# Four of sixteen new sample states moved from the second FFN into the mixer, and one weight quarter moved from a DMA to VectorE

## The chip, the cores and the metric

The kernel runs on one core of a Trainium2 chip. A core has five engines with a queue each: TensorE (PE in the profile; PEld is its weight load), VectorE (DVE), ScalarE (ACT), GpSimd (POOL) and SyncE (SP), which here only issues DMAs. POOL issues DMAs too, and it alone issues the accumulating ones, which add what they bring to what lies in the target. Each queue is worked off in order. The metric is the device time of one execution in microseconds (us); shorter is better.

## The reference

One inference step of a hybrid decoder trunk, in float32: half a SwiGLU FFN, a mixer, half a SwiGLU FFN, and a final RMSNorm. It runs for 512 prompt positions and for 8 sample sequences of one new token each; the kernel treats both together as 520 columns.

```python
h = h + 0.5 * _swiglu(_rms_norm(h, ffn1_norm), ffn1_w_gate, ffn1_w_up, ffn1_w_down)   # 1024 -> 2816 -> 1024
h = h + mixer(_rms_norm(h, mix_norm))      # in-projection, pooling, causal conv, SSD scan, gate, out-projection
h = h + 0.5 * _swiglu(_rms_norm(h, ffn2_norm), ffn2_w_gate, ffn2_w_up, ffn2_w_down)
y = _rms_norm(h, final_norm)
```

What the change touches is one output, the new recurrent state of the samples. For each sample b and each of 16 heads of 64 rows, with N = 128 state columns,

```
new_state[b] = exp(-dt * A) * state[b] + (dt * x) outer B[b]
y_sample[b]  = new_state[b] . C[b] + ...
```

The kernel holds a sample's state as 8 tiles of 128 x 128 (two heads in each). The names are `sdec` for the decay, one number for each partition, tile and sample, `sxdt` for dt * x, and a row of B that is broadcast to all partitions. The kernel computes `y_sample` without the new state, from the old one and from the dot product of B and C, so nothing on the chip reads the new state: it goes to the output `nss`.

## The kernel before

**Matrix products.** Every weight is split in two parts, a high part (a cast to the matmul's format, on ACT) and a low part (what the cast lost), and so are the activations. A product takes three matmuls: high x high, high x low, low x high (`mm3`, lines 146, 149 and 150). 520 columns are two halves of 260, one matmul each. The low part of a weight is either a subtraction on DVE (L136, L237, L384) or made by DMA: ACT copies the high part negated, and an accumulating DMA on POOL's queue adds the original from memory (`part_by_dma` L230, and L382).

**The FFNs.** Each FFN goes through 22 tiles of 128 hidden rows in chunks of 8, 8 and 6 (`CHUNKS`). After the first and the second chunk come four down products each, `Down(0,d)` and `Down(1,d)`; the last chunk's down products come at the end (`down_by_half`). A tile combines its two column halves and its two halves of the contraction with sums and differences, so that seven products do the work of eight (`product(f, p)`, p from 1 to 7); sums of weights are made on DVE (L412, L414, L415). The product with p = 4 uses one quarter of the weights; it is made late, in `quarter(f)`, and is multiplied within the next tile. `LOW_BY_DMA` lists the tiles whose quarter gets its low part by DMA: for the second FFN, tiles 0 to 6, 9 and 11.

Raw weights arrive over SP's queue into two buffers of 1 MB in turn, so a tile's load waits until the tile two before it has been split. The partial sums leave PSUM by copies on ACT (L476) and sums on DVE (L480, L485).

**The mixer.** Three strings, `CONV_PLAN`, `GATE_PLAN` and `LAST_PLAN`, give the order in which the program is written down: one letter and a number for each step. `b`, `x`, `p`, `z` are in-projections (24 units of weights), `A` and `B` the two halves of a scan step for a chunk of 128 positions and a group of heads (`ssd_a`, `ssd_b`), `s2` two sample steps (`sample`, L1088), `G` and `H` the gate, `o`, `g`, `h` out-projections, `n` a part of the second FFN's first tile that fills in. A planner then puts each engine's queue in order: in a simulated time it issues what is ready, the earliest written first. What is marked `keep_in_program_order` keeps its order among its like.

A sample step loads a row of C and half a sample's state (4 tiles, 256 KB) over SP, multiplies them on DVE (L1094), and sums each tile along its columns on ACT (L1097); that ACTIVATE's own output is not needed and goes to a tile `junk`, which shares its place (the tag "acc") with the FFNs' square sums.

**New sample states.** `new_states` (L1109) is a generator in the second FFN. Its 16 states are halves of samples, (b, g), 256 KB each. POOL's queue loads the row of B (64 KB) and the old state. Four ACTIVATEs write row x `sxdt` (L1139), four DVE instructions compute state x `sdec` + that (L1141), and a store goes out on POOL's queue (L1143). The loads run up to two states ahead, and the tile `room` has two places. `STATES` says when the generator moves on by one state: in `stream` (L534) the tuple's first member gives the number of states at each Down product by its d, the second lists tiles, and the third counts the first down products of the last chunk. The first call only loads. So before, the generator is started at tile 6, makes one state at each of the eight Down products, one each at tiles 17, 19, 20 and 21, and four at the end.

Of the kernel before, what the change touches and what calls it, by code (L numbers as in the profile page):

```python
# [10 lines left out]
F32 = mybir.dt.float32  # L11
F32R = mybir.dt.float32r
AF = mybir.ActivationFunctionType
ALU = mybir.AluOpType
# [3 lines left out]
P = 128  # L18
D = 1024
SEQ = 512  # L20
NS = 8
NT = SEQ + NS
# [12 lines left out]
CHUNKS = (8, 8, 6)  # L35
LOW_ON_DVE = ((2, 0), (3, 0), (KF - 1, 1))
ON_ACT = 4
STATES = ((1, 1, 1, 1), (6, 17, 19, 20, 21), 4)
LOW_BY_DMA = {1: (2, 3, 4, 5, 6), 2: (*range(7), 9, 11)}

CONV_PLAN = (
    "b0 b1 d0 b2 b3 x0 x1 v0 d1 x2 x3 d2 X0 p0 y0 c0 A0 k0 p1 x4 m0 x5 B0 c1 p2 m1 A1 x6 c2 A2 B1 x7 X1 m2 A3"
)
GATE_PLAN = (
    "z0 B2 A4 z1 B3 p3 z2 B4 s2 z3 c3 A5 s2 z4 m3 B5 s2 A6 z5 e0 s2 G0 z6 A7 z7 B6 s2 o0 H0 s2 o1 B7 s2 o2 s2 G1 "
    "o3 g0 g1 H1 g2 g3"
)
LAST_PLAN = "h0 h2 h1 n0 h3 n1 n2 n3"
SAMPLE_U = 3 + SEQ
# [14 lines left out]
def tile_trunk_step(ctx: ExitStack, tc: tile.TileContext, ins: dict, outs: dict):  # L64
    nc = tc.nc
# [5 lines left out]
    act = ctx.enter_context(tc.tile_pool(name="act", bufs=1, side="left"))  # L71
# [184 lines left out]
    class Ffn:  # L256
# [277 lines left out]
        def stream(self, before, last_chunk):  # L534
            tiles = []
            for f in range(self.direct, KF):
                tiles.append(f)
                if f and f <= self.folded and f % CHUNKS[0] == 0:
                    tiles.extend(Down(f // CHUNKS[0] - 1, d) for d in range(KD // 2))
            prev = None  # L540
            for t in tiles:
                for _ in range(STATES[0][t.d] if not isinstance(t, int) else t in STATES[1]):
                    next(self.states, None)
                self.product(t, 1)
                if prev is not None:
                    self.product(prev, 4)
                for k, p in enumerate((2, 5, 6, 3, 7) if t in (2, KF - 1) else (5, 6, 3, 7, 2)):
                    if k == 1 and prev is not None:
                        self.close(prev)
                    self.product(t, p)  # L550
                self.gates(t)
                if t == 5 and self.later:
                    with queued(*ends[1:]):
                        self.later.pop()()
                prev = t
            self.product(KF - 1, 4)
            with tc.high_priority():
                self.close(KF - 1)
            wd = before()
            if wd is None:  # L560
                self.down(len(CHUNKS) - 1, self.folded, KF, last_chunk)
            else:
                self.down_by_half(len(CHUNKS) - 1, self.folded, last_chunk, wd)
# [48 lines left out]
        def down_by_half(self, c, lo, after, wd):  # L612
            n = KF - lo
            banks, units = {}, []
            for d in range(KD):
                if d < STATES[2]:
                    next(self.states)
# [46 lines left out]
    wx1, g1 = pool("wx1", "right"), pool("g1", "right")  # L664
# [116 lines left out]
    g2 = f2["ffn"].gp = pool("g2", "left")  # L781
# [16 lines left out]
    todo, late = [], []  # L798
# [49 lines left out]
def mixer(tc, ins, outs, e):  # L848
    nc = tc.nc
    cst, act, wp, tmp, dr, pool = (e[x] for x in ("cst", "act", "wp", "tmp", "dr", "pool"))  # L850
# [4 lines left out]
    xh, xl, _, r = nx2[0]  # L855
    xa = e["xa"][0]
    mp = pool("mx", "right")
# [191 lines left out]
    sdec = cst.tile([P, NX, NS], F32, tag="sdec", name="sdec")  # L1049
    sxdt = cst.tile([P, NX, NS], F32, tag="sxdt", name="sxdt")  # L1050
    ysm = mp.tile([P, NX, NS], F32, tag="ysm", name="ysm")
    sbc = mp.tile([P, 2, NS], F32, tag="sbc", name="sbc")
    junk = act.tile([P, NT], F32, tag="acc", name="junk")[:, :P]
    scr_bc = dr.tile([NS, 512], F32, name="scr_bc")

    def rows_bc(b, a, g):
        return scr_bc.rearrange("b (a g n) -> b a g n", a=2, g=2)[b, a, g].unsqueeze(0).to_broadcast([P, P])
# [30 lines left out]
    def sample(b, g):  # L1088
        cb = tmp.tile([P, HB], F32, tag="ta", name=f"cb{b}{g}")[:, :P]
        nc.sync.dma_start(out=cb, in_=rows_bc(b, 1, g))  # L1090
        h0 = mp.tile([P, 4, P], F32, tag="h0", bufs=4, name=f"h0_{b}{g}")
        nc.sync.dma_start(out=h0, in_=ins["state_ssm"][:, b, 4 * g : 4 * g + 4])
        tc.keep_in_program_order(
            nc.vector.tensor_tensor(out=h0, in0=h0, in1=cb.unsqueeze(1).to_broadcast([P, 4, P]), op=ALU.mult))  # L1094
        for q in range(4):
            tc.keep_in_program_order(
                nc.scalar.activation(out=junk, in_=h0[:, q], func=AF.Copy,  # L1097
                                     accum_out=ysm[:, 4 * g + q, b : b + 1]))

    def sample_y(g):  # L1100
# [8 lines left out]
    def new_states(room):  # L1109
        spare = [room.rearrange("p (a q n) -> p a q n", a=2, q=4)] * 2  # L1110

        def load(b, g):
            if "hg" in f2:
                br = f2["hg"].tile([P, P], F32, tag="br", bufs=3, name=f"br{b}{g}")
                hs = f2["hg"].tile([P, 4, P], F32, tag="hs", bufs=3, name=f"hs{b}{g}")
            else:
                br = tmp.tile([P, HB], F32, tag="ta", name=f"br{b}{g}")[:, :P]
                hs = spare[g][:, b % 2]
            tc.keep_in_program_order(nc.gpsimd.dma_start(out=br, in_=rows_bc(b, 0, g)))
            tc.keep_in_program_order(nc.gpsimd.dma_start(out=hs, in_=ins["state_ssm"][:, b, 4 * g : 4 * g + 4]))  # L1120
            return br, hs

        todo = [(b, g) for g in range(2) for b in range(NS)]
        ahead = []
        for i, (b, g) in enumerate(todo):
            if not ahead:
                ahead.append(load(b, g))
            yield
            while i + len(ahead) < len(todo) and len(ahead) < 2 + 2 * ("hg" in f2):
                ahead.append(load(*todo[i + len(ahead)]))  # L1130
            br, hs = ahead.pop(0)
            if "hg" in f2:
                o = f2["hg"].tile([P, 4, P], F32, tag="so", bufs=2, name=f"so{b}{g}")
            else:
                o = bank(f"so{b}{g}").rearrange("p (q n) -> p q n", q=4)
            for q in range(4):
                j = 4 * g + q
                tc.keep_in_program_order(
                    nc.scalar.activation(out=o[:, q], in_=br, func=AF.Copy, scale=sxdt[:, j, b : b + 1]))  # L1139
                tc.keep_in_program_order(  # L1140
                    nc.vector.scalar_tensor_tensor(out=hs[:, q], in0=hs[:, q], scalar=sdec[:, j, b : b + 1],  # L1141
                                                   in1=o[:, q], op0=ALU.mult, op1=ALU.add))
            tc.keep_in_program_order(nc.gpsimd.dma_start(out=outs["nss"][:, b, 4 * g : 4 * g + 4], in_=hs))  # L1143
        yield

    e["f2"]["states"] = new_states


# [137 lines left out]
    def outs_a():  # L1286
        nc.sync.dma_start(out=outs["ncp"], in_=ncp)
        nc.sync.dma_start(out=outs["ncs"], in_=sconv)
        nc.sync.dma_start(out=outs["npp"], in_=npp)
        nc.sync.dma_start(out=outs["nps"], in_=spool)  # L1290
# [20 lines left out]
        "h": lambda j: wout(cats[1], 2, j, fin),  # L1311
        "n": fill,
        "e": lambda j: outs_a(),
    }

    def run(plan):
# [98 lines left out]
```

## Time and profile before

| | before |
|---|---|
| time, median of 3 runs | 964.78 us (963.81 to 965.73) |
| profiled execution | 965.28 us |
| its span, first to last instruction | 963.5 us |
| granted TensorE clock | 0.997 |
| busy PE / DVE / ACT / POOL | 99% / 88% / 66% / 15% |
| mixer, by TensorE's work | about 340 to 615 us |
| second FFN, tiles 1 to 8 | about 618 to 699 us |
| Down(0,0) to Down(0,3) | about 700 to 742 us |
| tiles 9 to 16, then Down(1,0) to Down(1,3) | about 742 to 824, to 865 us |

The profile is of one execution. A row of the timeline has the start, the duration, engine and line, output and inputs, and in brackets how long the engine stood idle before it and for whom. A matmul is shown with a modelled end and overlaps the next one, so a gap is read from start to start. A busy TensorE in a stretch can still have lost time; the count of matmuls in it says more.

### The profile page before, as it was taken

How to read it: one execution, taken by the hardware profiler on the slowest of the kernel's cores; microseconds unless marked ns; L12 is line 12 of the kernel's file. 1: busy time of each engine (PE TensorE's matmuls, PEld its weight loads, DVE VectorE, ACT ScalarE, POOL GpSimd, SP SyncE). 2: the span in 40 equal slices, each digit the busy share in tenths (PEclk: the TensorE clock that was granted, in tenths of full speed). 3: DMA queues.
4: the chain of work that ended last, by engine and by line, in shares of the span. 5: the costliest groups of instructions: out<-in, count | busy, mean ns of one | idle time of the engine just before them, and what ended most of it. 6: DMA issues, size and time to landing. Idle time of an engine off the chain costs nothing.

```text
span 963.5 us, 19707 instructions
## 1 busy us (share of the span) xinstructions
PE 949.7 (99%) x7676; PEld 930.3 (97%) x7676; DVE 850.3 (88%) x1456; ACT 640.7 (66%) x1208; POOL 142.9 (15%) x228
## 2 busy tenths in 40 slices
PE   9999999999999999999999999999999999999995
PEld 8999999999999999999999999999999999999995
DVE  6899899998997788789978897999889999999886
ACT  7777656676566455485676565677676676766763
POOL 0111101001010001055241000112112101122120
PEclk9999999999999999999999999999999999999998
DMA  7665654545534243362353333447656655666642
GB/s 210 182 167 145 152 156 111 138 136 143 163 112 129 73 142 110 94 199 92 117 159 121 115 117 114 117 121 166 170 154 178 154 146 147 166 192 174 187 141 90
DMA packets 53631, 137.30 MB, mean 142 GB/s; under 512 B 7641, under 2 KB 15769, under 8 KB 53537
## 3 DMA queue, kind: packets, MB, share of 16 engines
q1 hardware_dynamic: 39840, 104.18, 33.4%
q0 software_dynamic: 13424, 31.73, 17.2%
q8 instruction: 60, 0.98, 0.4%
q14 instruction: 35, 0.28, 0.1%
q10 hardware_dynamic: 272, 0.13, 0.0%
HBM read 128.67 MB, written 7.34 MB: 141 GB/s over the span
## 4 chain that ended last, share of the span: by engine, by line
PE 29%; DVE 11%; issue 4%; ACT 3%; DMA 3%; POOL 0%; DVEq 0%; ACTq 0%; POOLq 0%
PE A L150 3%; PE A L146 3%; PE A L149 3%; PE BE L149 3%; PE BE L146 2%; PE BE L150 2%; DMA raw<-in_w2d 2%; PE wo L146 2%; PE wo L150 2%; PE wo L149 2%; PE dh L150 1%; PE dh L146 1%; PE dh L149 1%; ACT junk L1097 1%; PE P L295 1%
## 5 line engine op out<-in xcount | busy, mean ns | idle before, releaser
L476 ACT COPY ac<-A 128x260 f32<-128x260 f32 x85 | 31.7, 373 | 34.8 <-PE A L150 33.6
L412 DVE TENSOR_TENSOR s<-raw 128x1024 f32<-128x1024 f32 x39 | 47.5, 1219 | 2.9 <-DMA raw<-in_w1gu 1.3
L476 ACT COPY ac<-BE 128x260 f32<-128x260 f32 x41 | 15.4, 376 | 30.0 <-PE BE L150 29.0
L146 PE MATMUL inx<-xh_mx,whi_inx 128*128 128x260 f32 x112 | 31.8, 284 | 0.0
L149 PE MATMUL inx<-xl_mx,whi_inx 128*128 128x260 f32 x112 | 31.6, 282 | 0.0
L150 PE MATMUL inx<-xh_mx,wlo_inx 128*128 128x260 f32 x112 | 31.6, 282 | 0.0
L977 DVE SCALAR_TENSOR_TENSOR A<-U,h,A 128x544 f32<-128x544 f32 x36 | 28.9, 802 | 1.3 <-ACT A L975 0.9
L295 PE MATMUL P<-x,raw 128*128 128x260 f32 x128 | 28.6, 384 | 0.0
L295 PEld LDWEIGHTS P<-x,raw 128*128 128x128 f32 x128 | 24.2, 191 | 4.0 <-DMA raw<-in_w1gu 0.4
L146 PE MATMUL wo<-catg,whi_wo 128*128 128x260 f32 x96 | 27.7, 289 | 0.0
L150 PE MATMUL wo<-catg,wlo_wo 128*128 128x260 f32 x96 | 27.2, 284 | 0.0
L149 PE MATMUL wo<-catg,whi_wo 128*128 128x260 f32 x96 | 27.1, 282 | 0.0
L1097 ACT ACTIVATE junk<-h 128x128 f32<-128x128 f32 x64 | 19.8, 309 | 10.5 <-DVE h L1094 9.0
L1139 ACT ACTIVATE so<-br,sxdt 128x128 f32<-128x128 f32 x64 | 22.5, 375 | 4.6 <-DVE room L1141 4.6
L150 PE MATMUL A<-xth_f,qs 128*128 128x260 f32 x84 | 23.8, 283 | 0.7 <-DMA qs<-in_w2gu 0.7
L146 PE MATMUL A<-xth_f,qs 128*128 128x260 f32 x84 | 23.8, 284 | 0.0
L1240 DVE TENSOR_TENSOR h<-wo,h 128x260 f32<-128x260 f32 x48 | 19.0, 416 | 5.4 <-PE wo L150 5.4
L149 PE MATMUL A<-xtl_f,qs 128*128 128x260 f32 x84 | 23.7, 282 | 0.0
L237 DVE TENSOR_TENSOR gs<-gq,gs 128x780 fp32r<-128x780 f32 (+1 forms) x28 | 23.2, 827 | 0.4 <-ACT gs L236 0.4
L146 PE MATMUL inz<-xh_mx,whi_inz 128*128 128x260 f32 x80 | 22.9, 287 | 0.0
L149 PE MATMUL inz<-xl_mx,whi_inz 128*128 128x260 f32 x80 | 22.7, 283 | 0.0
L150 PE MATMUL inz<-xh_mx,wlo_inz 128*128 128x260 f32 x80 | 22.6, 283 | 0.0
(2529 smaller groups left out, 4745.6 us busy)
## 6 DMA issues: line engine op xcount, KB each, us to landing
raw<-in_w2gu SPq DMA_DIRECT2D x44, 512.0 KB, 4.1
raw<-in_w1gu SPq DMA_DIRECT2D x41, 512.0 KB, 4.2
raw<-in_w_in SPq DMA_DIRECT2D x24, 512.0 KB, 3.6
raw<-in_w1d SPq DMA_DIRECT2D x16, 512.0 KB, 4.5
raw<-in_w2d SPq DMA_DIRECT2D x16, 512.0 KB, 4.8
raw<-in_w_out SPq DMA_DIRECT2D x12, 512.0 KB, 3.7
ab<-scr_acs SPq DMA_DIRECT2D x8, 512.0 KB, 5.0
h<-in_state_ssm SPq DMA_DIRECT2D x16, 256.0 KB, 3.3
```

Of the source, the lines that this page charges most:

```text
L146: first = nc.tensor.matmul(ps, whi, xhi, start=start, stop=False, **kw)
L149: nc.tensor.matmul(ps, whi, xlo, start=False, stop=False, **kw)
L150: nc.tensor.matmul(ps, wlo, xhi, start=False, stop=stop, **kw)
L237: low = nc.vector.tensor_tensor(out=lo, in0=s, in1=hi.bitcast(F32), op=ALU.subtract)
L295: mm = nc.tensor.matmul(self.banks[f, u][b][:, :HB], ws(self.raw[f][:, u], j + 4 * q), xg[:, slot[q]], start=j == q == 0, stop=j == 3 and ...
L412: nc.vector.tensor_tensor(out=s1, in0=diag, in1=up0, op=ALU.add)
L476: self.copied = nc.scalar.copy(keep, out[:, :HB]).ins
L977: nc.vector.scalar_tensor_tensor(out=A[:, :n], in0=U[:, j : j + n], scalar=w(j), in1=A[:, :n], op0=ALU.mult, op1=ALU.add)
L1097: nc.scalar.activation(out=junk, in_=h0[:, q], func=AF.Copy, accum_out=ysm[:, 4 * g + q, b : b + 1]))
L1139: nc.scalar.activation(out=o[:, q], in_=br, func=AF.Copy, scale=sxdt[:, j, b : b + 1]))
L1240: nc.vector.tensor_tensor(out=h[:, d, hs], in0=ps[:, :HB], in1=h[:, d, hs], op=ALU.add)
```

## The change

Four of the 16 states, b = 0 to 3 of the first half, are no longer made in the second FFN. A new generator, `first_states`, makes them in the mixer, moved on by the new step `t` in `GATE_PLAN`, nine times. For each state SP loads the row of B and the old state; after a projection ACT scales the row by `sxdt` into a tile `o`, and the old state by `sdec` in place; POOL issues an accumulating DMA from `o` to the state; after another projection SP stores it, and goes on with the next state's loads into the same two tiles. `o` takes the place that `junk` had, and so the sample steps' sums now write their unneeded output over their own input.

In the second FFN the generator starts with the fifth state, at tile 15. `STATES[0]` is now indexed by the chunk: none at Down(0,d), one at each Down(1,d). Tiles 17, 19, 20, 21 and the last down products make the same states as before. Tile 9 leaves `LOW_BY_DMA`, so the low part of its quarter is subtracted on DVE.

```diff
-STATES = ((1, 1, 1, 1), (6, 17, 19, 20, 21), 4)
-LOW_BY_DMA = {1: (2, 3, 4, 5, 6), 2: (*range(7), 9, 11)}
+FIRST = 4
+STATES = ((0, 1), (15, 17, 19, 20, 21), 4)
+LOW_BY_DMA = {1: (2, 3, 4, 5, 6), 2: (*range(7), 11)}
 
 GATE_PLAN = (
-    "z0 B2 A4 z1 B3 p3 z2 B4 s2 z3 c3 A5 s2 z4 m3 B5 s2 A6 z5 e0 s2 G0 z6 A7 z7 B6 s2 o0 H0 s2 o1 B7 s2 o2 s2 G1 "
-    "o3 g0 g1 H1 g2 g3"
+    "t0 z0 t0 B2 A4 z1 t0 B3 p3 z2 t0 B4 s2 z3 t0 c3 A5 s2 z4 t0 m3 B5 s2 A6 z5 t0 e0 s2 G0 z6 t0 A7 z7 B6 t0 s2 o0 H0 s2 o1 "
+    "B7 s2 o2 s2 G1 o3 g0 g1 H1 g2 g3"
 )
...
-                for _ in range(STATES[0][t.d] if not isinstance(t, int) else t in STATES[1]):
+                for _ in range(STATES[0][t.c] if not isinstance(t, int) else t in STATES[1]):
...
-    junk = act.tile([P, NT], F32, tag="acc", name="junk")[:, :P]
...
-                nc.scalar.activation(out=junk, in_=h0[:, q], func=AF.Copy,
+                nc.scalar.activation(out=h0[:, q], in_=h0[:, q], func=AF.Copy,
                                      accum_out=ysm[:, 4 * g + q, b : b + 1]))
...
-        todo = [(b, g) for g in range(2) for b in range(NS)]
+        todo = [(b, g) for g in range(2) for b in range(NS)][FIRST:]
...
+    def first_states():
+        for b in range(FIRST):
+            br = mp.tile([P, P], F32, tag="mb", name=f"mb{b}")
+            hs = mp.tile([P, 4, P], F32, tag="mh", name=f"mh{b}")
+            nc.sync.dma_start(out=br, in_=rows_bc(b, 0, 0))
+            nc.sync.dma_start(out=hs, in_=ins["state_ssm"][:, b, :4])
+            yield
+            o = act.tile([P, NT], F32, tag="acc", name=f"mo{b}")[:, : 4 * P].rearrange("p (q n) -> p q n", q=4)
+            for q in range(4):
+                nc.scalar.activation(out=o[:, q], in_=br, func=AF.Copy, scale=sxdt[:, q, b : b + 1])
+                nc.scalar.activation(out=hs[:, q], in_=hs[:, q], func=AF.Copy, scale=sdec[:, q, b : b + 1])
+            nc.gpsimd.dma_start(out=hs, in_=o, accum_op=ALU.add)
+            yield
+            nc.sync.dma_start(out=outs["nss"][:, b, :4], in_=hs)
+
+    firsts = first_states()
...
+        "t": lambda j: next(firsts, None),
```

## The prediction

> **What bounds the kernel now.** I read the page's head first, then the busy time in equal stretches, then the waits of TensorE, then the timeline and the chain of work around each wait.
>
> ```profile
> span 963.5 us, 19707 instructions
> PE 949.7 (99%) x7676; PEld 930.3 (97%) x7676; DVE 850.3 (88%) x1456; ACT 640.7 (66%) x1208; POOL 142.9 (15%) x228
> ...
> 660.00:680.00 20.00, 20.00 (x169) 20.00 (x168) 18.33 (x28) 15.86 (x27) 4.59 (x6) 1.00 0.69 176
> 680.00:700.00 20.00, 19.30 (x161) 19.09 (x160) 16.48 (x27) 12.63 (x22) 2.88 (x4) 1.00 0.62 161
> 700.00:720.00 20.00, 19.93 (x166) 19.72 (x165) 19.47 (x35) 15.37 (x30) 2.86 (x4) 1.00 0.67 172
> 720.00:740.00 20.00, 19.04 (x154) 18.46 (x153) 17.05 (x33) 11.70 (x24) 5.08 (x8) 1.00 0.66 165
> 740.00:760.00 20.00, 19.34 (x161) 19.13 (x161) 18.60 (x30) 12.56 (x22) 3.72 (x5) 1.00 0.75 192
> 760.00:780.00 20.00, 20.00 (x169) 20.00 (x169) 18.53 (x30) 15.06 (x26) 2.56 (x3) 1.00 0.52 133
> ```
>
> The columns of a stretch are its length, then PE, weight loads, DVE, ACT and POOL with their instruction counts, the granted clock, the DMA share and GB/s. TensorE is the bound: 99% busy, clock 1.00, and a full stretch of the second FFN holds 169 matmuls, one per 20/169 = 0.118 us. The four stretches from 680 to 760 hold 161+166+154+161 = 642 instead of 676. The missing 34 are 34 x 0.118 = 4.0 us (a little of that can be lost records). That place is tiles 7 and 8, the first chunk's down products Down(0,0) to Down(0,3), and tiles 9 and 10. The timeline shows where TensorE stood: each pair is the matmul before a gap and the one after it.
>
> ```profile
> 693.10 0.28 PE L149 MATMUL A<-xtl_f,shi_8d 128*128 128x260 f32 x1
> 694.09 0.39 PE L150 MATMUL A<-xth_f,slo_8d 128*128 128x260 f32 x1 [0.70 <-DVE slo_8d L136]
> ...
> 720.40 0.28 PE L149 MATMUL A_Down(c=0, d=2)_8948<-gs,whi_Down(c=0, d=2)a 128*128 128x260 f32 x1
> 721.00 0.39 PE L150 MATMUL A_Down(c=0, d=2)_8948<-gs,wlo_Down(c=0, d=2)a 128*128 128x260 f32 x1 [0.32 <-DMA wlo_Down(c=0, d=2)a<-in_w2d]
> ...
> 733.98 0.28 PE L150 MATMUL A_Down(c=0, d=2)_8948<-gs,qs 128*128 128x260 f32 x1
> 734.91 0.39 PE L146 MATMUL BE_Down(c=0, d=3)_9083<-gs,shi_Down(c=0, d=3)c 128*128 128x260 f32 x1 [0.65 <-ACT BE_Down(c=0, d=3)_9083 L476]
> ...
> 753.85 0.28 PE L149 MATMUL A<-xtl_f,qs 128*128 128x260 f32 x1
> 754.80 0.39 PE L150 MATMUL A<-xth_f,qs 128*128 128x260 f32 x1 [0.66 <-DMA qs<-in_w2gu]
> ```
>
> From start to start, less one step of 0.12, the four lose 0.87, 0.48, 0.81 and 0.83 us: 2.99. The rest of the 4.0 is slow steps after each gap and smaller hesitations. Four gaps, four suppliers: DVE, an accumulating DMA, ACT, and the quarter of tile 9 by DMA. What stood ahead of each supplier:
>
> ```profile
> 682.58 0.84 POOL L1120 DMA_DIRECT2D room<-in_state_ssm  x1
> 684.43 6.79 DMA raw<-in_w2d
> 711.93 0.57 POOL L1119 DMA_DIRECT2D br<-scr_bc  x1 [6.96 <-ACT so L1139]
> 712.91 0.84 POOL L382 DMA_DIRECT2D wlo_Down(c=0, d=2)a<-in_w2d  x1 [0.41 <-ACT BE_Down(c=0, d=1)_8816 L476]
> 732.41 0.38 ACT L1139 ACTIVATE so<-br,sxdt 128x128 f32<-128x128 f32 x1
> 733.66 0.38 ACT L1139 ACTIVATE so<-br,sxdt 128x128 f32<-128x128 f32 x1
> 734.48 0.38 ACT L476 COPY BE_Down(c=0, d=3)_9083<-A_Down(c=0, d=3)_9082 128x260 f32<-128x260 f32 x1
> 746.77 7.99 DMA qs<-in_w2gu
> ```
>
> **The change, part by part.** The sum is made on the profiled execution: 965.28 us, of which the span is 963.5. The median of the runs is 964.78, 0.5 lower.
>
> *Gap 1 (0.87).* slo_8d stood in DVE's queue behind the sums of Down(0,0), which waited for raw weights that took 6.79 us. Just ahead POOL issued the load of sample state 1: 256 KB, and 64 KB of row B. At the 161 GB/s of that stretch 320 KB are 2.0 us of traffic, at twice that rate 1.0; both exceed 0.87. These loads are gone, so I take this gap as closed.
>
> *Gap 2 (0.48).* The low half of Down(0,2) is an accumulating DMA on POOL's queue; it was issued 712.91 and the matmul that reads it started at 721.00, 8.1 us later. Ahead of it in the queue a state's br load waited 6.96 us for ACT, right behind it a 256 KB store competed. Both are gone: closed.
>
> *Gap 3 (0.81).* TensorE waited for a copy on ACT, and ACT had a state's scaling in between. By the next rows each costs a step of 2.44/8 = 0.305 us. The two rows at 732.41 and 733.66 are about 0.6; I leave 0.2 of this gap standing.
>
> *Gap 4 (0.83).* Tile 9's quarter: today ACT casts and negates, POOL issues, and the sum lands 7.99 us later. After: cast, then one subtraction on DVE (0.68 us by the row below). The issue at 746.77 is later than the cast, so DVE has some 7 us until 754 and 0.68 of its own to do. DVE is 18.60 of 20 busy there, and loses 16 state updates of 0.338 (5.4 us) over these tiles. I take the new cost as zero; without that relief DVE would be late by at most its 0.68. The raw tile is now released by DVE and not by ACT, so tile 11's load starts a little later; other tiles of this stream already work so.
>
> *Started at tile 15 and not at 6.* The first load pair (two POOL issues) moves from the stretch 660:680, where it cost TensorE nothing (169 matmuls), to tile 15. Zero, with gap 1's 0.87 as the far end, since that is what a pair of loads ahead of the raw weights went with.
>
> ```profile
> L1139 ACT ACTIVATE so<-br,sxdt x64: 349/376/403, 700.7 to 930.2; 128x128 f32<-128x128 f32 x64
> L1141 DVE SCALAR_TENSOR_TENSOR room<-room,sdec,so x52: 331/338/348, 705.9 to 927.7; 128x128 f32<-128x128 f32 x52
> 925.44 2.44 ACT L1139 ACTIVATE so<-br,sxdt 128x128 f32<-128x128 f32 x8
> L237 DVE TENSOR_TENSOR qs<-raw,qs 128x512 fp32r<-128x512 f32 x21 | 14.3, 681 | 0.4 <-ACT qs L236 0.4
> qs<-in_w2gu POOLq DMA_DIRECT2D x8, 256.0 KB, 6.6
> out_nss<-room POOLq DMA_DIRECT2D x13, 256.0 KB, 4.5
> ...
> 455.00:475.00 20.00, 20.00 (x172) 18.14 (x172) 19.34 (x40) 14.13 (x28) 7.11 (x9) 1.00 0.31 99
> 475.00:490.00 15.00, 15.00 (x128) 14.07 (x128) 12.56 (x28) 8.83 (x20) 8.25 (x8) 1.00 0.41 130
> 490.00:505.00 15.00, 15.00 (x130) 14.07 (x130) 10.81 (x20) 14.32 (x45) 3.76 (x5) 1.00 0.53 162
> 505.00:522.00 17.00, 17.00 (x145) 17.00 (x145) 14.06 (x29) 11.44 (x43) 2.13 (x2) 1.00 0.41 138
> ...
> 468.27 1.22 DVE L1193 TENSOR_TENSOR ab<-ab,scm 128x1024 f32<-128x1024 f32 x1
> 472.02 1.09 PE L1208 MATMUL yd<-ab,xdt 128*64 128x128 f32 x16
> ...
> 477.25 0.33 SPq L142 DMA_DIRECT2D raw<-in_w_in  x1
> 501.33 1.03 ACT L134 CAST whi_inz<-raw 128x1024 fp32r<-128x1024 f32 x1
> ```
>
> *Added to the mixer, ACT.* Eight scalings per state, 32 in all, 32 x 0.305 = 9.8 us. They fall between z0 and the end of the scan, 455 to 522, where ACT is busy 48.7 of 67.0 and idle 18.3: they fit. One state is a burst of 2.44 us; the tightest supplier I found is the decay product, done at 468.27+1.22 = 469.49 and read by TensorE at 472.02, 2.5 us to spare. So I take zero. TensorE is full here (67.00 of 67.00), so a gain is excluded; the upper bound is all 9.8 on the path, and I keep 1.0 of it in the likely range.
>
> *Added, POOL and the DMAs.* Four accumulating issues at the 0.84 of the row above are 3.4 us on POOL, busy 21.3 of 67.0. Their transfers, SBUF to SBUF, appear nowhere before; the nearest rows are the accumulating quarters (6.6 us median) as the high end and a plain 256 KB store (4.5) as the low one. I take 6.6. Nobody on TensorE's path reads the result.
>
> The Trainium skill, "SBUF — State Buffer", in the box on the trap that DVE blocks DMA, says that a DMA issued from GpSimd can wait for its descriptors while DVE holds the shared port, about 3.1 us against 0.62; four such issues would be an estimated 12.4 us of POOL instead of 3.4. The issues here, beside a DVE busy 17 to 19.5 us of 20, took 0.57 to 0.84, so the trace does not show that rule at work.
>
> *Added, SP.* Eight loads and four stores, 0.33 us each as the raw row shows: 4.0 us of issue. What waits counts more. A store waits for its accumulating DMA, and the next state's load, right behind it in the program, waits for that store to have left the same tile (4.5). Behind them in SP's queue stand the raw weights, the decay rows and the sample states. The last z weights are issued at 477.25 and cast only at 501.33: 24 us to spare, less a transfer of 6.79 at the slowest shown. The store is placed one projection (48 matmuls x 0.118 = 5.7 us) after the scaling, a little less than the 6.6 assumed. Zero taken.
>
> *Sample dot products in place.* The same 64 ACTIVATEs with the same shapes, other target: zero, and the spread of such an instruction (376 to 403) excludes more than 64 x 0.03 = 1.7 us of ACT, off the path.
>
> Sum: 4.0 less 0.2 of gap 3, less 0.3 of small hesitations left: 3.5 gained, 0 paid. 965.28 - 3.5 = 961.8 for the profiled execution, 964.78 - 3.5 = 961.3 for the median.
>
> **The rivals.**
>
> *A. The gaps come back.* The second chunk's down products carry the same four states and TensorE is full there:
>
> ```profile
> 705.00:745.00 40.00, 39.04 (x321) 38.46 (x320) 36.52 (x67) 26.67 (x52) 7.60 (x12) 1.00 0.72 188
> 825.00:865.00 40.00, 40.00 (x334) 40.00 (x333) 37.23 (x67) 27.03 (x53) 8.10 (x13) 1.00 0.70 183
> ```
>
> With equal DVE, ACT and DMA loads, 321 matmuls against 334. So states alone do not make gaps; the first chunk reaches its down products with less lead, and with the states gone some other thing may be late at the same place. Then only gap 4 is sure: 964.78 - 0.9 = 963.9, no difference that can be measured. Against it: three of the four suppliers had a state's instruction or transfer directly in front.
>
> *B. SP's queue turns into the brake: slower.* If the accumulating DMAs land later than the store's place, SP stands (7.99, the slowest shown, less 5.7: 2.3 us), then 4.5 for the load behind, 6.8 per state. A sample state's load issued that late is waited for by DVE, whose sample products are pinned in order, so the scan behind them is late too. Against a margin of 2.5 us at the decay product that leaves 4.3 per state; over the three states that have a load behind a store, 12.9 us, minus 3.5 gained: 964.78 + 9.4 = 974.2. It decides from 3.5 us in all, or 1.2 per state. For it: each link is in program order. Against: the order in each queue is planned by simulated readiness, and the weights lead by more than 17 us.
>
> In a sentence apart: the Trainium skill, "DMA: Bandwidth & Descriptors", section on the anatomy of one DMA, gives 2.0 us plus bytes over 436 GB/s, an estimated 2.6 for 256 KB, by which no store would wait and B would fall; the accumulating rows here took 6.6 and 8, so the measurement decides and B stays.
>
> *C. Half of it.* The mixer's bursts cost 2.0 (two of the four over the 2.5 us margin by about a microsecond) and the gaps close: 963.3.
>
> **How the numbers follow.** A change of 0.2%, 1.9 us, is about what a measurement of this kernel can tell from none; its runs spread 963.81 to 965.73. My forecast 0.66, with its own range 960.3 to 962.8 (all 4.0 and half a microsecond of spread; or the 1.0 of the mixer and 0.5). A 0.12, C 0.07, B 0.15. Faster is the forecast and a share of C (0.70), same A and the rest of C (0.15), slower B (0.15). The range for 8 in 10 runs from 960.0 to 966.6: up over C and A, and into B where it costs 5.3 in all.
>
> **What would show it.** Right: 169 matmuls in each 20 us from tile 7 to tile 10, no gap with the four releasers above, no L1139 and no state DMA before tile 15; tile 9's quarter on DVE, ready before TensorE asks; TensorE still full in the mixer, with the 32 scalings in what was ACT's idle time. Wrong: TensorE gaps between 455 and 620 released by the scan or by a weight cast, or DVE waiting for a sample state; or gaps in Down(0,0) to Down(0,3) with new releasers.

## The result: slower, and where the profile of the changed kernel shows it

The changed kernel takes 971.32 us (median of 6 runs, 970.02 to 972.64) beside 964.62 for the kernel before (6 runs, 963.81 to 965.73). The ratio is 1.0069, with a 95% interval of 1.0056 to 1.0082: slower by 6.7 us, where 3.5 us of gain were forecast. The profiled execution took 970.94 us, 969.2 of it the span.

The stretches and TensorE's waits of the changed kernel, in the mixer (columns as in the prediction: length, PE, weight loads, DVE, ACT, POOL with counts, granted clock, DMA share, GB/s):

```profile
440.00:460.00 20.00, 17.79 (x140) 16.22 (x139) 17.78 (x28) 12.48 (x30) 10.43 (x19) 0.95 0.52 166
460.00:480.00 20.00, 17.26 (x129) 16.11 (x129) 14.75 (x35) 19.53 (x43) 5.04 (x9) 0.88 0.52 153
...
458.10:461.51 3.41, 3.41 (x18) 3.41 (x17) 3.41 (x13) 2.69 (x8) 1.78 (x4) 0.50 0.40 71
475.17:478.58 3.41, 3.05 (x14) 3.06 (x15) 1.37 (x4) 3.38 (x8) 0.49 (x3) 0.50 0.65 151
...
PE px L1179 <- ACT X L980: 2.7, 1, 2.7
PE pm L150 <- DVE catp L1034: 0.8, 1, 0.8
PE inz L147 <- DVE E L1235: 0.8, 1, 0.8
PE pm L147 <- ACT catp L1033: 0.6, 1, 0.6
```

The same stretches of the kernel before:

```profile
440.00:460.00 20.00, 20.00 (x172) 19.07 (x171) 19.55 (x39) 11.45 (x24) 12.74 (x19) 1.00 0.24 84
460.00:480.00 20.00, 20.00 (x173) 18.14 (x172) 19.24 (x38) 12.26 (x29) 5.35 (x8) 1.00 0.42 137
```

The loss sits in these 40 us: 269 matmuls instead of 345. TensorE is idle for 4.9 us (the four waits), and after the pauses its granted clock falls to half for 3.41 us, twice, at most 0.50 x 3.41 x 2 = 3.4 us more. Together 8.3. The start of the second FFN says the same:

```profile
618.14 0.28 PE L147 MATMUL A<-xth_f,whi_1a 128*128 128x260 f32 x1
```

In the trace before, this matmul starts at 609.90: 8.24 us later now. The last matmuls of tile 21 are 6.5 us late (923.04 beside 916.58); so up to there the second FFN gave back 1.8.

What stood ahead of TensorE's suppliers: first ScalarE's own rows (in brackets its idle time and who ended it), then SyncE's, then the waits of both (us in all, times, longest).

```profile
437.88 1.28 ACT L1155 ACTIVATE mo<-mb,sxdt 128x128 f32<-128x128 f32 x4 [3.89 <-DMA mh<-mo]
457.32 1.28 ACT L1156 ACTIVATE mh<-mh,sdec 128x128 f32<-128x128 f32 x4 [3.19 <-DMA mh<-in_state_ssm]
474.85 0.63 ACT L980 ACTIVATE X<-A 128x512 f32<-128x512 f32 x1
...
449.86 0.34 SPq L1159 DMA_DIRECT2D out_nss<-mh  x1
452.03 0.42 SPq L1151 DMA_DIRECT2D mh<-in_state_ssm  x1
452.55 0.38 SPq L1181 DMA_DIRECT2D ab<-scr_acs  x1
481.94 0.32 SPq L1181 DMA_DIRECT2D ab<-scr_acs  x1
...
SPq L1159 <- DMA mh<-mo: 29.6, 4, 9.3
...
ACT mh L1156 <- DMA mh<-in_state_ssm: 4.5, 2, 3.2
```

ScalarE scales a state, GpSimd's DMA adds it up, SyncE stores it, SyncE loads the next state into the same place, ScalarE waits for that load. The last conv silu (X), behind two such waits, runs at 474.85 instead of 464.68; ScalarE, with 19.53 us of 20 busy from 460 to 480, has no room left to catch up. The four stores hold SyncE for 29.6 us. ScalarE's wait of 2.5 us ahead of its scalings at 449.87 has no releaser in the trace, but it ends as an accumulating DMA lands: the store that waits for the same DMA goes out at 449.86. In the kernel before the same loads of the decay rows, and that silu, stand here:

```profile
448.36 0.37 SPq L1165 DMA_DIRECT2D ab<-scr_acs  x1
473.15 0.32 SPq L1165 DMA_DIRECT2D ab<-scr_acs  x1
...
464.68 0.63 ACT L979 ACTIVATE X<-A 128x512 f32<-128x512 f32 x1 [1.05 <-DVE A L977]
```

The first of the two is 4.2 us late (452.55), behind a store and a state load; at the second (481.94) TensorE itself, whose yd frees the rows' place, is as late, so that one proves nothing. Two more things add to the delay. The transfer itself took longer (5.9 us from issue to landing for the rows issued at 452.55, 4.4 for those issued at 448.36 before); no run separates what the added traffic alone costs. And GpSimd's queue is worked off in order too: the third accumulating DMA stood there 5.70 us for its scaling, until 458.90, and `we`, the first step on the rows, ran right behind it at 459.50, a microsecond after the rows had landed. The scalings run at other times than the prediction had them (455 to 522): all of them from 424.0 to 472.6, while the convolution still needs ScalarE.

### The profile page after: what moved, and what is told of

It is laid out like the page before. It is cut to its first block, busy times and chain, and to the rows that moved or that the text cites. A ratio compares the mean times of both kernels' runs of the same rounds, so it can differ in the third digit from the quotient of the medians.

```text
span 969.2 us, 19723 instructions
## 1 busy us (share of the span) xinstructions
PE 952.4 (98%) x7676; PEld 933.1 (96%) x7676; DVE 848.8 (88%) x1441; ACT 644.2 (66%) x1225; POOL 135.2 (14%) x219
## 4 chain that ended last, share of the span: by engine, by line
PE 40%; DVE 6%; DMA 3%; ACT 2%; issue 1%; DVEq 0%; POOL 0%; SPq 0%; POOLq 0%; ACTq 0%
PE A L151 3%; PE A L147 3%; PE A L150 3%; PE wo L147 2%; PE wo L151 2%; PE wo L150 2%; PE BE L150 2%; PE BE L151 2%; PE BE L147 2%; PE inz L147 1%; PE inz L151 1%; PE inz L150 1%; DMA raw<-in_w2d 1%; PE dh L151 1%; PE dh L147 1%
## 5 line engine op out<-in xcount | busy, mean ns | idle before, releaser
L1097 ACT ACTIVATE h<-h 128x128 f32<-128x128 f32 x64 | 18.9, 296 | 12.9 <-DVE h L1094 12.9
L137 DVE TENSOR_TENSOR tlo<-raw,thi 128x1024 fp32r<-128x1024 f32 (+1 forms) x14 | 16.9, 1205 | 8.3 <-ACT thi L135 8.2
```

Of the source, the lines that this page charges most:

```text
L137: low = nc.vector.tensor_tensor(out=l, in0=src, in1=h.bitcast(F32), op=ALU.subtract)
L1097: nc.scalar.activation(out=h0[:, q], in_=h0[:, q], func=AF.Copy, accum_out=ysm[:, 4 * g + q, b : b + 1]))
```

## The experiments

The theories: **1**, ScalarE's queue stands behind the states' DMAs. **2**, the added ScalarE work is itself too much. **3**, which is rival B: SyncE's queue stands behind the stores, and what is loaded behind them comes late. A mixer loss is the shift of the second FFN's first matmul against the first trace of before, less the shift at the end of the first FFN (317.06 there); in the changed kernel 8.24 + 0.05 = 8.3. All ratios are to the kernel before, on the same chip.

| run | us | ratio (95%) | mixer loss, us |
|---|---|---|---|
| changed kernel | 971.32 | 1.0069 (1.0056 to 1.0082) | 8.3 |
| no states in the mixer | 964.28 | 0.9996 (0.9984 to 1.0008) | -0.5 |
| scalings alone | 965.04 | 0.9992 (0.9982 to 1.0002) | -0.6 |
| DMAs alone | 966.88 | 1.0019 (1.0008 to 1.0031) | 3.3 |
| scalings behind the silu | 973.77 | 1.0085 (1.0070 to 1.0101) | 8.3 |
| late stores | 969.40 | 1.0045 (1.0032 to 1.0057) | 5.5 |
| late stores, behind the silu | 969.87 | 1.0052 (1.0038 to 1.0066) | 6.4 |
| two places | 968.85 | 1.0033 (1.0020 to 1.0046) | 4.0 |
| two places, tile 9 by DMA | 968.35 | 1.0034 (1.0022 to 1.0047) | 3.7 |
| decay rows first, tile 9 by DMA | 965.87 | 1.0016 (1.0007 to 1.0025) | 3.0 |
| samples first, tile 9 by DMA | 966.72 | 1.0016 (1.0007 to 1.0025) | 3.5 |
| scalings alone, behind the silu, tile 9 by DMA | 963.57 | 0.9987 (0.9978 to 0.9996) | -0.2 |
| no states in the mixer, tile 9 by DMA | 963.88 | 0.9984 (0.9975 to 0.9992) | -0.5 |
| tile 9's edit alone | 965.75 | 1.0012 (1.0003 to 1.0021) | 0.0 |
| before, once more | 965.14 | 1.0003 (0.9994 to 1.0012) | 0.4 |

The last row sets the scale: a second trace of the same kernel differs by 0.4 us in the loss.

### The parts: no states, the scalings alone, the DMAs alone

**No states in the mixer**: all nine `t0` steps are taken out of `GATE_PLAN`, so four of the 16 states are not made at all.

> The changed kernel without its four sample states in the mixer (they are left out of the output nss: its first four samples of half 0 are not written). Everything else of the change stays, tile 9's quarter on VectorE included. If the mixer's +8.2 us come from these states, by whatever road: no shift of TensorE's steps against the kernel before up to tile 1 of FFN2 (within 0.3 us), then the 3.1 us won between tile 1 and tile 11, less the 1.2 us of small new gaps behind it: 961.5 to 963 us. If they come from elsewhere in the change (the sample dot products' scaling in place, another planned order): the shift of 4 us or more at the second z unit stays, and the time is 967 or more.

0.9996, and no mixer loss: all of it comes from the four states. But the gain is not there either (below).

**The scalings alone.**

```diff
-            br = mp.tile([P, P], F32, tag="mb", name=f"mb{b}")
+            br = ident
...
-            nc.sync.dma_start(out=br, in_=rows_bc(b, 0, 0))
-            nc.sync.dma_start(out=hs, in_=ins["state_ssm"][:, b, :4])
...
-                nc.scalar.activation(out=hs[:, q], in_=hs[:, q], func=AF.Copy, scale=sdec[:, q, b : b + 1])
-            nc.gpsimd.dma_start(out=hs, in_=o, accum_op=ALU.add)
+                nc.scalar.activation(out=hs[:, q], in_=ident, func=AF.Copy, scale=sdec[:, q, b : b + 1])
...
-            nc.sync.dma_start(out=outs["nss"][:, b, :4], in_=hs)
```

> The changed kernel with only the 32 scalings of the four states on ScalarE, from a constant tile; their loads, accumulating DMAs and stores are left out, and so are four states of the output nss. Theory 1 (ScalarE's queue stands behind the states' DMAs, 8.4 us of waits on the state load and on the accumulating DMA between 436 and 490): these waits are gone, the wait of the transpose px for the last conv silu falls from 2.7 to under 0.8, TensorE's shift at the FFN is at most +2.5 us, time 961.5 to 965. Theory 2 (the 9.8 us of scalings and two more table loads of 1.28 fill ScalarE ahead of the last conv silus): the shift stays at +6 or more, time 968 to 971.

0.9992, no loss, and no wait of TensorE between 440 and 640. Theory 2 falls, with one reservation: with no DMA to wait for, the 32 scalings ran from 411.8 to 444.2, and not from 424.0 to 472.6 as in the changed kernel, so it is shown for that place only.

**The DMAs alone**: the two lines of scalings and the tile `mo` out, the accumulating DMA reads `ident`.

> The changed kernel with the loads, accumulating DMAs and stores of the four states in the mixer but without their 32 scalings: the accumulating DMA adds a constant tile, so four states of the output nss are wrong in value. Theory 3 (rival B of the prediction: SyncE's queue stands behind the stores, 29.6 us of waits on the accumulating DMAs, and what is loaded behind them comes late): shift of +4 us or more at the second z unit, time 966 or more. Theories 1 and 2 (both need ScalarE): shift of at most 1 us at the FFN, time 961.5 to 963.5.

A loss of 3.3 us without one added ScalarE instruction. It is not the loss of the changed kernel, though: with nothing to wait for on ScalarE the four states ran from 357 to 399. The SyncE queue shows what it was instead.

```profile
398.67 0.34 SPq L1155 DMA_DIRECT2D out_nss<-mh  x1
399.54 0.44 SPq L957 DMA_DIRECT2D scr_dt<-dts  x1
403.26 1.31 SPq L1061 DMA_DIRECT2D sdt<-scr_dt  x2
...
412.98 1.99 SPq L1177 DMA_DIRECT2D ab<-scr_acs  x3
...
SPq L1155 <- DMA mh<-ident: 16.7, 2, 8.5
SPq L1177 <- DMA scr_acs<-ach: 4.2, 1, 4.2
```

The last store waited 8.5 us. Behind it scr_dt went out at 399.54 (before: 393.12), its reading back stands right ahead of the write of the decay rows, and SyncE waited 4.2 us for that write (before: 0.6). The rows are loaded at 412.98 instead of 407.45. The order is that of theory 3 with another victim, but the link is argued and not shown: the write was issued only 0.6 us later than before (406.25 for 405.63) and then took longer to land, and why was not tried.

### The place on ScalarE

**The scalings behind the last conv silu**: the loop over q stands in `with queued(*held["silu"]):`.

> The changed kernel, complete, with the states' scalings put behind the last conv silu in ScalarE's queue. Theories 1 and 2 with the place as the cause: the wait of px for the last silu (2.7 us) goes, and the pauses of TensorE at 454 to 458 with it; what is left are the scalings beside the z and out stages, where ScalarE had 18.3 us of 67 idle: 961.5 to 964.5. If the place is not the cause (the work is too much wherever it stands in the mixer): the pauses come back at z or at the out units, behind the catp casts or the decay product, and the time stays at 968 or more.

Neither: the pauses at 454 to 458 go, but the time is 973.77, and TensorE stands 3.2 us at 503 for catp. SyncE's queue there:

```profile
475.00 0.34 SPq L1160 DMA_DIRECT2D out_nss<-mh  x1
477.02 0.33 SPq L1151 DMA_DIRECT2D mh<-in_state_ssm  x1
...
477.94 0.37 SPq L1182 DMA_DIRECT2D ab<-scr_acs  x1
...
POOL we L1186 <- DMA ab<-scr_acs: 12.0, 3, 9.3
```

The decay rows went out at 473.15 before; here a store and the loads behind it keep them until 477.94, and GpSimd waits 9.3 us for them (4.5 before). ScalarE, too, stands 3.34 us for a state's load, at 493.09, ahead of the cast for catp. This other place on ScalarE only moves the stop to another stage.

### The queue: stores behind the decay rows

**Late stores**: load, scaling and store become three steps of the plan, and a store, with the next loads, is queued behind the newest load of the decay rows. In the plan the scalings of the second to fourth state move back, too.

```diff
+        held["ab"] = nc.sync.dma_start(out=ab, in_=scr_acs[...]).ins
...
+        with queued(held["ab"]):
+            nc.sync.dma_start(out=outs["nss"][:, b, :4], in_=mst[b][1])
+            if b + 1 < FIRST:
+                state_in(b + 1)
```

> The changed kernel, complete, with each state's store and the next state's loads put behind the next load of the decay rows (ab) in SyncE's queue. Theory 3 (a store waits 5 to 9 us for its accumulating DMA at the head of SyncE's queue, and the decay rows behind it come 4 us late): the decay rows are issued when the states are left out (near 448, 464, 474, 487), the loss in the mixer falls from 8.2 us to at most 2.5 (ScalarE's own part was 0.6 in the run of its scalings alone, and one state still stands ahead of the last silu), time 965 to 967. Theory 1 (ScalarE stands on the states' DMAs in its own queue, whatever SyncE does): ScalarE's waits on mh and mo stay at 6 us or more and the time at 969 or more.

**The same with the scalings behind the silu.**

> The same with the scalings also behind the last conv silu in ScalarE's queue. Theory 3: the 9.3 us wait of GpSimd's we for the decay rows, which the run with the scalings behind the silu shows, goes, and so does TensorE's 3.2 us pause at catp: time 964.5 to 966.5. Theory 1: ScalarE still waits for the state's load and for the accumulating DMA between the z units, and the pause at catp stays: 970 or more.

Between the two: 969.40 is a time that theory 1 had (969 or more), but ScalarE's waits for the states' DMAs are down to 3.5 us, where theory 1 had 6 or more; 969.87 lies between. The new order is 0.24% or 2.3 us faster at the change's own place (1.0069 to 1.0045) and 0.33% or 3.2 us behind the silu (1.0085 to 1.0052). In the first pair the scalings moved as well (426.4 to 507.6, where the changed kernel has 424.0 to 472.6), and the intervals touch; in the second they run from about 468 to 508 both times, so that one shows what the queue's order is worth. In the run with late stores the four loads of the decay rows between 450 and 490 come 1.5 to 3.1 us later than in the kernel before, 1.4 of it lost already in this trace's first FFN, and now the loop through the one place shows by itself. ScalarE and SyncE of the first of them:

```profile
489.85 0.33 SPq L1187 DMA_DIRECT2D ab<-scr_acs  x1
496.07 0.34 SPq L1164 DMA_DIRECT2D out_nss<-mh  x1
496.46 0.43 SPq L1150 DMA_DIRECT2D mb<-scr_bc  x1
...
500.82 1.28 ACT L1158 ACTIVATE mo<-mb,sxdt 128x128 f32<-128x128 f32 x4 [3.24 <-DMA mb<-scr_bc]
502.01 1.03 ACT L135 CAST whi_inz<-raw 128x1024 fp32r<-128x1024 f32 x1
...
PE yd L1230 <- DVE ab L1215: 1.2, 1, 1.2
```

SyncE holds the store until 496.07, then loads the next row, ScalarE stands 3.24 us for it, the weight cast behind it is late, VectorE's subtraction and the decay product after that, and TensorE stands 1.2. TensorE's other pauses in this trace are 1.4 us for the silu and 1.1 and 0.6 for VectorE. Theories 1 and 3 are links of one loop.

**Two places**, on top of the last version: `mh` gets two buffers (room from the token decay's scratch, laid into `hst` and `mb`), and the next state is loaded right behind the scalings; with tile 9's edit, and without it.

```diff
-        mst[b] = mp.tile([P, P], F32, tag="mb", ...), mp.tile([P, 4, P], F32, tag="mh", name=f"mh{b}")
+        mst[b] = mp.tile([P, P], F32, tag="mb", ...), mp.tile([P, 4, P], F32, tag="mh", bufs=2, name=f"mh{b}")
...
         nc.gpsimd.dma_start(out=hs, in_=o, accum_op=ALU.add)
+        if b + 1 < FIRST:
+            state_in(b + 1)
```

> The changed kernel, complete, with a second place for the mixer's sample state (2 KB a partition, found by letting the token decay's scratch lie in the state buffer hst and in the row's place), the next state loaded as soon as the last one's scalings are done, stores behind the decay rows, scalings behind the last conv silu. The run with late stores showed ScalarE standing 3.2 us on the row that SyncE could load only behind the store, and a weight cast behind it (theory 1 and theory 3 as one loop: accumulate, store, load, scale, all through one place). If that loop is the cost: no ScalarE wait on a state's load of over 1 us, ScalarE's weight casts on time, mixer loss at most 1.5 us, time 964.5 to 966. If the load of ScalarE and the queues themselves is the cost, place or no place: loss of 4 us or more as with one place (969.4 to 969.9).

> The same with tile 9's quarter left to the accumulating DMA, as before the change. The run of tile 9's edit alone was 0.75 us slower than before, with pauses at Down(1,3) and at tile 18's last quarter in its trace that neither trace of before has. If that edit causes them: they are gone, and this is 0.5 to 1.2 us faster than the same kernel with the edit; about 964, the best complete version. If they are drawn by chance: no difference.

968.85 and 968.35, so part of the loop only. The ratios of the two are alike (1.0033 and 1.0034): tile 9's edit costs nothing that shows in this pair, where 0.5 to 1.2 us were expected. One load of the decay rows is still late, because the plan put the first store ahead of it:

```profile
475.21 0.34 SPq L1168 DMA_DIRECT2D out_nss<-mh  x1
...
478.15 0.40 SPq L1189 DMA_DIRECT2D ab<-scr_acs  x1
...
POOL we L1193 <- DMA ab<-scr_acs: 9.4, 3, 6.4
```

**Decay rows first**: each store one load of the decay rows later (`w0` moves from behind `A5` to behind `A6`, and so on), and the loads of the third and fourth state no longer right behind the scalings but behind those stores; as the control **the same scalings with every added DMA left out**.

```diff
-z3 c3 A5 w0 s2 z4 u1 m3 B5 s2 A6 w1 z5 u2 e0 s2 G0 z6 A7 w2 z7 B6 u3 s2 o0 H0
+z3 c3 A5 s2 z4 u1 m3 B5 s2 A6 w0 z5 u2 e0 s2 G0 z6 A7 w1 z7 B6 u3 s2 o0 w2 H0
...
-        if b + 1 < FIRST:
-            state_in(b + 1)
+        if b == 0:
+            state_in(1)
...
+            if b + 2 < FIRST:
+                state_in(b + 2)
```

> The changed kernel, complete, with two places for the state, tile 9's quarter by DMA, and every store and state load now behind the next load of the decay rows but one: with two places alone SyncE still issued the third load of the rows at 478.2 instead of 473.8, behind a store and a state load, and GpSimd's we waited 6.4 us for it. Theory 3: that load is back at 474 and the next at 487 to 488, the wait of we is under 3 us, and the mixer's loss falls from 3.5 us to at most 1.5: 965 to 966. If ScalarE's 9.8 us of scalings in a shorter stretch (470 to 510) is what is left: the rows are on time, but the loss stays at 3 us or more, 967.5 to 969.

> The 32 scalings alone behind the last conv silu, without loads, accumulating DMAs and stores (four states of the output nss are left out), tile 9's quarter by DMA. It takes SyncE and the DMAs out of the same late place: if they were the cost there, the mixer loses at most 1 us and the time is 963 to 965, as with the scalings alone at the change's own place (0.6 us); if the scalings themselves are too much behind the silu, pauses at catp and at the state products stay, loss 3 us or more, 966.5 to 968.

```profile
473.79 0.32 SPq L1191 DMA_DIRECT2D ab<-scr_acs  x1
474.81 0.34 SPq L1168 DMA_DIRECT2D out_nss<-mh  x1
487.32 0.33 SPq L1191 DMA_DIRECT2D ab<-scr_acs  x1
...
POOL we L1195 <- DMA ab<-scr_acs: 3.6, 3, 2.8
...
PE wo L147 <- DVE E L1245: 1.1, 1, 1.1
PE inz L147 <- DVE hst L1241: 0.7, 1, 0.7
```

The rows are back at 473.79 and 487.32, the wait of we falls from 6.4 to 2.8, and the time by 0.18%, to 965.87. The two intervals touch (1.0022 and 1.0025), and the mixer losses of the two traces differ by 0.7 us only. The control, with the same 32 scalings behind the silu, is 0.9987, as fast as the kernel with no states in the mixer at all (0.9984). With no DMA to wait for, its scalings are done from 468.8 to 482.6, where the complete version has them from 468.5 to 503.9. So the loss hangs on the states' DMAs and on who stands behind them; the scalings by themselves cost nothing at either place where they were tried.

**Samples first**: the last two stores also behind the loads of the sample dot products.

> The changed kernel, complete, as with the decay rows first, and the last two states' stores behind the loads of the sample dot products too. There the store that waits 4 to 6 us from 488 is still ahead of the loads of cb and h (issued at 495.7 instead of 489.6 with the scalings alone), and pauses at 510.6 (0.7 us) and 555.8 (1.1 us) are left. Theory 3 for these loads as well: cb and h are issued at 490 to 491, the two pauses go, the mixer loses at most 1 us, 963.6 to 965.2, level with or just under before. If the pauses come from elsewhere they stay, and the time is that of the rows first, 965.9.

1.0016 again. The 0.7 us pause went, the 1.1 us at wo (for VectorE's E) stayed, and 0.9 us came at the gate's norm. What the last 0.3% between 1.0016 and 0.9987 is, some 2.8 us, **stays open**: in both traces only the 1.1 us pause is seen, beside one of 0.2 us that the control has too, and it is VectorE that ends it. No complete version beats the kernel before.

### What the change could have won

**Tile 9's edit alone; the kernel before, once more; no states in the mixer with tile 9 by DMA.**

```diff
-LOW_BY_DMA = {1: (2, 3, 4, 5, 6), 2: (*range(7), 9, 11)}
+LOW_BY_DMA = {1: (2, 3, 4, 5, 6), 2: (*range(7), 11)}
```

> The kernel before with tile 9's quarter on VectorE and nothing else. The prediction's gap 4 (0.83 us) says 964.0 with no other gap in its place. If gaps of this kind fall where a DMA happens to be late in one execution, as the runs with and without the states in the mixer suggest (four different places in four traces): within 0.3 us of before.

> The kernel before, profiled once more. If the four pauses of TensorE in the second feed-forward (0.87, 0.48, 0.81, 0.83 us) belong to the kernel, they stand at the same steps. If the two that wait for a DMA (0.48 and 0.83) are drawn anew in each execution, they stand elsewhere or not at all, and the two that wait for VectorE or ScalarE stay.

> The changed kernel without the four states in the mixer (left out of the output nss) and with tile 9's quarter by DMA: it only has four sample states fewer in the second feed-forward than before, the whole gain that the change could buy. By the prediction's gaps 1 to 3 it is 2.2 us under before, 962.8. If those pauses were drawn by chance in the one execution profiled (the second trace of before has one pause where the first has four): 963.5 to 964.8.

The two traces of the kernel before, 680 to 760 us (first the one that the prediction was made from, then the second), each with its waits of TensorE after 640:

```profile
680.00:760.00 80.00, 77.59 (x635) 76.39 (x634) 71.60 (x122) 52.26 (x95) 14.54 (x21) 1.00 0.67 173
PE A L150 <- DVE slo_8d L136: 0.7, 1, 0.7
PE A L150 <- DMA qs<-in_w2gu: 0.7, 1, 0.7
PE BE_Down(c=0, d=3)_9083 L146 <- ACT BE_Down(c=0, d=3)_9083 L476: 0.6, 1, 0.6
...
PE A_Down(c=0, d=2)_8948 L150 <- DMA wlo_Down(c=0, d=2)a<-in_w2d: 0.3, 1, 0.3
```

```profile
680.00:760.00 80.00, 79.59 (x654) 78.75 (x654) 74.07 (x125) 53.85 (x99) 14.53 (x21) 1.00 0.68 174
PE A L150 <- DMA qs<-in_w2gu: 0.9, 2, 0.7
...
```

None of the four pauses comes again in its size at its step: there are two waits for a quarter by DMA, the larger at another step (0.7 us, until 671.80), and 0.2 us until 754.18, where the first trace had 0.7. The line left out of both is a wait of 0.6 us near the end, which both traces have. Between the first FFN2 matmul and tile 21 the second trace is 1.7 us shorter than the first: as much as the 1.8 that the changed kernel seemed to gain there. The runs alone tell the gain: 0.16% or 1.5 us (0.8 to 2.4) for four states fewer, and a loss of 0.12% or 1.2 us (0.3 to 2.0) for tile 9's edit. The sum is nothing, which is what the kernel with no states in the mixer shows (0.9996). Why tile 9's edit costs here, and not between the two versions with two places, is not settled: the pauses at Down(1,3) and tile 18 that its trace has stand in that of the kernel with no states in the mixer and tile 9 by DMA too, which hasn't the edit.

## Why the prediction was wrong, by its own steps

- **Added, SP** is the step that failed. It said "Zero taken". It named the decay rows among what stands behind a store, but gave a margin only for the raw weights (24 us; that one held). At the decay product it had 2.5 us of margin itself, and the rows came 4.2 late (4.8 with the scalings behind the silu, 477.94 for 473.15). Holding the stores back behind them took 3.2 us off where the scalings kept their place (behind the silu), and 2.3 with the scalings moved as well; moving stores and state loads once more took another 0.18%.
- **Rival B** is what happened in its mechanism: SyncE stands at the stores, and what is loaded behind them is late. That 971.3 comes near its 974.2 is in part luck, for its terms were other ones. It had SyncE stand 2.3 us at a store and 4.5 for the load behind it, 6.8 in all; the stores stood 7.4 on average (29.6 / 4) while the next states' loads stood only 0.7 in all behind the stores, which landed in 2.0 (median). And it put a store's wait down to a slow accumulating DMA, but these took 3.3, 3.3, 3.3 and 5.7 us, 15.6 of the 29.6; the other 14.0 had passed before GpSimd issued them, because the scalings were late. It had the victims wrong: not the raw weights or a sample state on VectorE, but the decay rows and ScalarE, which waits in order for the next state's load.
- **Added to the mixer, ACT**: zero is right as a price of the work (0.9992 and 0.9987 for the scalings alone). The place was wrong: 424 to 473, not 455 to 522; the place in the written plan isn't the place in the queue. And the step priced durations only, not what ScalarE would wait for: 4.5 us for the states' loads and 3.9 for an accumulating DMA between 436 and 490, and the 2.5 that end as another one lands.
- **Added, POOL and the DMAs**: 6.6 us assumed from issue to landing; measured 3.3 in the changed kernel, 5.7 at most (below, its DMA issues: count, size, median us to landing). "Nobody on TensorE's path reads the result" was the wrong question: two queues wait for it. One reading there is off: of the issues beside a "DVE busy 17 to 19.5", the one at 682.58 lies in a stretch with 16.48.

```profile
mh<-mo POOLq DMA_DIRECT2D x4, 256.0 KB, 3.3
```

- **Gaps 1 to 4** (3.5 us): the places were read rightly off the trace, but as the kernel's own. They belong to one execution. Gaps 1 to 3 were worth 1.5 (0.8 to 2.4): less than the 2.7 that the sum took with its hesitations, while the 2.2 by their rows are not excluded; **gap 4** came out with the other sign (1.2 lost for 0.8 gained).
- **Started at tile 15** and **sample dot products in place**: no loss shown (0.9996 with both in).
- **Rival A** holds for the second FFN: with the mixer's cost taken out the gain is too small to tell from none. **Rival C**'s bursts weren't the cause.
- The list of what would show it wrong had the right stretch (455 to 620) and the scan as releaser. The falling clock, up to 3.4 of the 8.3 us, was in no sum.

## What to carry to other kernels

A DMA's price is not its transfer but who stands behind the instruction that waits for it: for each queue that a new store, load or accumulation enters, list the loads behind it and their margins, and give a load that feeds a scan its place ahead of any store that waits. A loop over one buffer (scale, accumulate, store, load) ties all the queues it passes through together, so give it a second place and enough distance. Pauses under 1 us in one trace are not yet the kernel's: take a second trace of the same kernel before you price their removal.

## What the runs showed of the hardware

**The clock after a pause.** In these traces the granted clock is 1.00 or 0.50. In the changed kernel it falls to 0.50 at 458.10 and at 475.17, for 3.41 us each, and again near the end, at 963.27. These times lie 5 and 143 times 3.413 us apart, so the clock is set for one window of 3.41 us after the other, and a pause doesn't move the windows. Here are the two windows ahead of the half clock in the changed kernel, then two that follow each other in the run with late stores behind the silu, counted back from its own fall at 961.86:

```profile
454.69:458.10 3.41, 1.81 (x13) 1.38 (x13) 3.41 (x8) 0.78 (x3) 0.00 (x0) 1.00 0.89 356
471.76:475.17 3.41, 1.02 (x9) 0.81 (x7) 2.52 (x6) 3.38 (x6) 0.86 (x1) 1.00 0.27 49
```

```profile
497.65:501.06 3.41, 2.06 (x18) 1.85 (x16) 2.15 (x6) 3.17 (x19) 0.00 (x0) 1.00 0.76 253
501.06:504.48 3.42, 2.15 (x14) 1.76 (x14) 2.72 (x5) 3.40 (x7) 1.27 (x1) 1.00 0.72 228
```

In the first two TensorE stood 1.60 us (3.41 - 1.81) and 2.39 us, and the next window ran at 0.50. In the run with the scalings behind the silu it stood 2.59 us from 500.89 to 504.30, and the half clock followed as well. In the last two it stood 1.35 and 1.27, because a border between windows falls into its pause of 2.1 us (499.71 to 501.78); the clock stayed at 1.00. In all 16 traces no window with 1.39 us of standing or less was followed by half clock (the 1.39 in the run with the DMAs alone, 421.03 to 424.44), and every one with 1.60 or more was; where the limit lies between them is open. So it isn't the length of one pause that decides, but how much standing falls into one window, and one window at half clock costs TensorE up to 0.50 x 3.41 = 1.7 us more. The Trainium skill, "TensorE: Matmul & The Clock Gate", Part 1, says that the clock falls to half after an idle window of about 3.4 us, and that the windows run free of the kernel. The half clock, the length and the free windows agree; the windows that brought it here were not idle throughout, though, but held 1.02 and 1.81 us of matmuls.

**An accumulating DMA** of 256 KB from SBUF to SBUF landed 3.3 us after its issue (median; 5.7 at most in the changed kernel, 6.9 with the decay rows first), less than the quarters from HBM (6.6). The estimate of 2.6 that the prediction worked out from the Trainium skill, "DMA: Bandwidth & Descriptors", section on the anatomy of one DMA, was the nearer one to the median, though no run reached it and the stores still waited: of their 29.6 us, 14.0 were the way round through the queues and not the transfer.
